# One core, a hybrid backbone block: the first down projection moved whole behind the first Strassen gate unit

## The chip, the cores and the metric

The kernel runs on one core of a Trainium2 chip. The metric is the device time of one execution in microseconds (us). Before the change it is 2523.57 us, the median of three runs (2523.08 to 2524.18). Views of the profile come from one profiled execution of the same kernel, which took 2524.79 us and whose instructions span 2523.1 us.

## The reference, cut to what matters

The block runs once (DEPTH = 1) on 512 tokens of width 2048. Two groups of recurrent heads, an output projection and a norm come first; the change touches only the channel mixer at the end:

```python
def conv_ffn(h, rows, cols, w_up, conv_w, conv_b, w_down):
    u = jnp.einsum('btd,df->btf', h, w_up)
    u_gate, u_val = jnp.split(u, 2, axis=-1)
    g = lax.conv_general_dilated(u_gate.reshape(b, rows, cols, D_FF), conv_w[:, :, None, :], ...
                                 feature_group_count=D_FF)
    g = g.reshape(b, t, D_FF) + conv_b
    return jnp.einsum('btf,fd->btd', jax.nn.silu(g) * u_val, w_down)
...
x = x + gt2 * conv_ffn(h2, rows, GRID_W, w_up, conv_w, conv_b, w_down)
return rmsnorm(x, g_final)
```

The inner width D_FF is 5504, that is 43 blocks of 128. The grid is 8 rows by 64 columns, and the convolution is 3x3 on each channel by itself.

## The kernel before, in words

All data lie with channels on the 128 partitions and the 512 tokens along the free dimension. Every product in float32 is made of three matrix products of parts: `split` copies a tile into a rounded `hi` on ScalarE (ACT, line 90) and takes the rest as `lo` on VectorE (DVE, line 91), and `mm3` (line 105) multiplies hi by hi, hi by lo and lo by hi. Weights come by DMA from the SP queue into four `raw` buffers and are split from there into two buffers for `hi` and two for `lo`, so that the DVE and ACT work for a weight chunk can run at most two chunks ahead of TensorE (PE).

The 43 blocks are cut into 11 groups (`QUADS`): group 0 has three blocks, the others four. A group q goes through four steps: the gate half of the up projection (`up_gate`, tile name ug), the convolution with its Silu (`convolve`, tile cv), the value half (`up_val`, tile uv) which is multiplied into the convolution's result and split (`product`, tiles gh and gl), and the down projection of these blocks (`down_sums`, tile dn). Down projections work in four blocks of 512 output channels; each block uses four PSUM banks, whose sums ACT scales into a staging tile `st` (line 1265) and a DMA from GpSimd's queue (POOL, line 1266) adds into the array x2d in HBM. The staging tiles come from a pool of three buffers.

Group 0 uses plain products (`unit`): per half 144 matmuls 512 wide, in three banks. Groups 1 to 10 use Strassen's scheme in a variant with seven products (`seven`: seven of the eight PSUM banks, 336 matmuls 256 wide per half), whose sums are put together by `four`: one copy on ACT and seven additions on DVE, in which the tiles u, v and t hold what is between. For this scheme the input tokens are needed in sums and differences as well: `token_sums(j)` and `token_last(j)`, j from 0 to 7, make them from the modulated tokens, and `token_last(j)` writes over a part of the operand that the plain products of group 0 read.

The SBUF tiles of this stage are sixteen named slots of one buffer each, y0 to y15 (`ytile(k, ...)`): two tiles in one slot exclude each other in time. First they hold the tokens x2; later u is y9, v is y11 and t is y13, convolution results are y8, y10, y12, y14, products y0 to y7. For group 0 the slots are written out by hand: the convolution results in y8, y9 and y13, the products gh and gl of its three blocks in y11 and y12, y15 and y7, y4 and y5.

The order on each engine's queue is fixed when the program is built: a planner takes, at each step of its own estimate of time, the ready instruction that comes first; program order sets the rank, and what stands under `tc.high_priority()` is ranked ahead. Engines then execute their queues strictly in order. On PE the order around the change is, from lines 1268 to 1285:

```python
up_gate(0)
...
convs = convolve(0); token_sums(2); up_val(0, convs)
...
down_sums(0, (0, 1), True)
for q in range(1, NQ):
    up_gate(q)
    down_sums(q - 1, (2, 3) if q == 1 else range(3) if q == NQ - 1 else range(4))
    up_val(q, convolve(q))
```

So the gate of group 0, the value of group 0, two blocks of down projection 0, the gate of group 1, the other two blocks of down projection 0, the value of group 1, the gate of group 2, and from there on down, value, gate in turn.

Of the kernel before, what the change touches and what calls it, by code (L numbers as in the profile page):

```python
# [11 lines left out]
F32 = mybir.dt.float32  # L12
F32R = mybir.dt.float32r
# [5 lines left out]
P = 128  # L19
HW = 256  # L20
D = 2048
KT = D // P
KP = KT // 2
T = 512
# [14 lines left out]
NQ = len(QUADS)  # L39
# [31 lines left out]
def block_kernel(ctx: ExitStack, tc: tile.TileContext, a: dict, out: bass.AP):  # L71
    nc = tc.nc
    V, S, G, PE = nc.vector, nc.scalar, nc.gpsimd, nc.tensor
# [9 lines left out]
    def mul(o, x, y):  # L83
        V.tensor_tensor(out=o, in0=x, in1=y, op=ALU.mult)
# [4 lines left out]
    def split(hi, lo, x):  # L89
        S.copy(hi, x)  # L90
        return V.tensor_tensor(out=lo, in0=x, in1=hi.bitcast(F32), op=ALU.subtract).ins  # L91
# [49 lines left out]
    def acc(name, shape=(P, T)):  # L141
        return (banks8[0] if banks8 else psA).tile(list(shape), F32, name=name, tag="acc")
# [5 lines left out]
    def ytile(k, name, shape=(P, T), dtype=F32):  # L148
        return yp.tile(list(shape), dtype, name=name, tag=f"y{k}")
# [56 lines left out]
    def unit_steps(src, name, xh, xl, accs, late=False, rates=None):  # L206

        n = len(accs)
        for kp in range(KP):
            if rates:  # L210
                rate[0] = rates[kp]
            wh, wl = load_split(src[kp], f"{name}_{kp}", w=P * n)
            if kp == 0 and late:

                for m, (ws, xs) in enumerate(((wh, xh), (wl, xh), (wh, xl))):
                    for k in range(2):
                        for i in range(n):
                            mm(accs[i], ws[:, k, P * i : P * i + P], xs[k], start=(m == 0 and k == 0), stop=False)
                continue
            for i in range(n):  # L220
                for kk in range(2):
                    k = 2 * kp + kk
                    mm3(accs[i], wh[:, kk, P * i : P * i + P], wl[:, kk, P * i : P * i + P],
                        xh[k], xl[k], k == 0, k == KT - 1)
                yield 1.36

    def unit(src, name, xh, xl, n=4, late=False, rates=None):

        accs = [acc(f"{name}_{i}") for i in range(n)]
        for _ in unit_steps(src, name, xh, xl, accs, late, rates):  # L230
            pass
        return accs
# [260 lines left out]
    cv = xp.tile([P, 32], F32, name="cv")  # L493
# [76 lines left out]
    for c0, n, hs, m in ((0, T, hx, gm[0]), (T, TC, hc, gm[1])):  # L570
        ps = psb(f"gm{c0}", (P, n))
        for k in range(KT):
            g = 32 * (k % 4)
# [417 lines left out]
    for h in range(1, 2 * H):  # L991
        if h + 1 < 2 * H:
            accs = [acc(f"a{h + 1}_{g}", BANKS[g]) for g in range(6)]
            steps = project_steps(h + 1, accs)
        else:
            rate[0] = 1.5
            accs = [acc(f"ga0_{i}") for i in range(4)]
# [16 lines left out]
    for g in range(4):  # L1014
        if g:
            accs = unit(a["w_gates"][g], f"ga{g}", *hx)
        for i in range(4):
            k = 4 * g + i
# [54 lines left out]
    for n in range(4):  # L1073
        pinned[0] = n == 3
        accs = unit(a["w_out"][n], f"wo{n}", yh, yl)
# [8 lines left out]
    with tc.high_priority():  # L1084
        _, r2 = token_rstd(sums2, rp, "rms2", idle=4)
# [12 lines left out]
    stp = pool(ctx, "stp", 3, waits="tile")  # L1098

    def operand(j, part, what, name, shape, dtype=F32R):  # L1100
        return bp.tile(list(shape), dtype, name=name, tag=f"b{part}{what}{j}")
# [6 lines left out]
    h2 = [[flat(b[k // 2][:, 2 * (k % 2) : 2 * (k % 2) + 2, :]) for k in range(KT)] for b in bq]  # L1108
# [15 lines left out]
    def token_sums(j):  # L1124

        k0, k1 = 2 * j, 2 * j + 1
        for k in (k0, k1):
            S.activation(x2[k], x2[k], AF.Identity, bias=modc[3][:, k : k + 1])
        sub(half(k0, 0), half(k0, 1), half(k0, 0))
        sub(half(k0, 1), half(k0, 1), half(k1, 1))  # L1130
        sub(half(k1, 1), half(k1, 1), half(k0, 0))
        split(flat(bt[0][j][:, 0:2, :]), flat(bt[1][j][:, 0:2, :]), x2[k0])
        sub(rest(j), half(k1, 1), half(k1, 0))
        split(bt[0][j][:, 2, :], bt[1][j][:, 2, :], half(k1, 1))
# [11 lines left out]
    gs = {}  # L1146
# [4 lines left out]
    def seven(src, name):  # L1151

        ps = [acc(f"{name}_{n}", (P, 2, HW)) for n in range(7)]
        for kp in range(KP):
            w = load_sums(src[kp], f"{name}_{kp}")
            for o, (g, s, b, c) in zip(ps, PRODUCTS):
                for m in range(2):
                    ms = slice(P * m, P * m + P)
                    mm3(o[:, m, :], w[g][0][:, s, ms], w[g][1][:, s, ms], b[0][kp][:, c, :], b[1][kp][:, c, :],
                        kp == 0 and m == 0, kp == KP - 1, skip_group_check=True)  # L1160
        return ps

    def four(ps, name, put):

        p1, p2, p4, p6, p7, p5, p3 = ps
        u, v = ytile(9, f"u_{name}", (P, 2, HW)), ytile(11, f"v_{name}", (P, 2, HW))
        with tc.high_priority():
            S.copy(u, p1)
            put(0, 0, u, p2, ALU.add)
            sub(u, u, p6)  # L1170
            sub(v, p7, u)
            put(1, 0, v, p4, ALU.subtract)
            put(1, 1, v, p5, ALU.add)
            sub(u, u, p5)
            put(0, 1, u, p3, ALU.add)

    def first_f(q):
        return 4 * q - 1 if q else 0
# [15 lines left out]
    def convolve(q):  # L1194
        convs = []
        for i in range(QUADS[q]):
            f = first_f(q) + i
            t = ytile((8, 9, 13)[i] if q == 0 else 8 + 2 * i, f"cv{f}")
            t3 = t.rearrange("p (r c) -> p r c", c=GW)
            for tap in range(9):  # L1200
                src = pads[:, i, tap // 3 : tap // 3 + ROWS, tap % 3 : tap % 3 + GW]
                w = cwt[:, f, tap : tap + 1]
                if tap == 0:
                    S.activation(t3, src, AF.Identity, scale=w, bias=cbt[:, f : f + 1])
                else:
                    V.scalar_tensor_tensor(out=t3, in0=src, scalar=w, in1=t3, op0=ALU.mult, op1=ALU.add)  # L1206
            S.activation(t, t, AF.Silu)
            convs.append(t)
        return convs

    def up_val(q, convs):

        def product(i):
            if q == 0:
                gh, gl = (ytile((11, 12, 15, 7, 4, 5)[2 * i + n], f"g{p}{i}", dtype=F32R) for n, p in enumerate("hl"))
            elif q == NQ - 1:
                gh, gl = (operand(4 + i, p, "t", f"g{p}{first_f(q) + i}", (P, T)) for p in "hl")
            else:
                gh, gl = (ytile(2 * i + n, f"g{p}{first_f(q) + i}", dtype=F32R) for n, p in enumerate("hl"))
            split(gh, gl, convs[i])  # L1220
            gs[first_f(q) + i] = (gh, gl)

        if q == 0:
            accs = unit(a["w_up3"][1], "uv0", *h2, n=3)
            with tc.high_priority():
                for i, ps in enumerate(accs):
                    mul(convs[i], convs[i], ps)
                    product(i)
        else:
            def put(mh, th, x, ps, op):  # L1230
                t = ytile(13, f"t{q}_{mh}{th}", (P, 2, HW))
                V.tensor_tensor(out=t, in0=x, in1=ps, op=op)  # L1232
                for i in range(2):
                    c = convs[2 * mh + i][:, HW * th : HW * th + HW]
                    mul(c, c, t[:, i, :])
                if (mh, th) in ((1, 1), (0, 1)):
                    for i in range(2):
                        product(2 * mh + i)

            four(seven(a["w_up4"][2 * q - 1], f"uv{q}"), f"uv{q}", put)  # L1240

    def down_block(q, blk, by_f=False):
        accs = [acc(f"dn{q}_{blk}_{i}") for i in range(4)]
# [13 lines left out]
    def down_sums(q, blks, by_f=False):  # L1257

        for blk in blks:
            accs = down_block(q, blk, by_f and blk == blks[0])  # L1260
            with tc.high_priority():
                for i in range(4):
                    k = 4 * blk + i
                    t = stp.tile([P, T], F32, name=f"st{q}_{k}", tag="st")
                    S.activation(t, accs[i], AF.Copy, scale=modc[5][:, k : k + 1])  # L1265
                    nc.gpsimd.dma_start(x2d[k], t, accum_op=ALU.add)  # L1266

    up_gate(0)
    st_p.close()
    banks8.append(pool(ctx, "psM", 8, PSUM, waits="tile"))  # L1270
    for j in reversed(range(3, KP)):
        token_sums(j)
    convs = convolve(0)
    token_sums(2)
    up_val(0, convs)
    for j in (1, 0):
        token_sums(j)
    for j in range(KP):
        token_last(j)
    down_sums(0, (0, 1), True)  # L1280
    for q in range(1, NQ):
        up_gate(q)
        down_sums(q - 1, (2, 3) if q == 1 else range(3) if q == NQ - 1 else range(4))
        up_val(q, convolve(q))
    down_sums(NQ - 2, (3,))

# [1 line left out]
    q = NQ - 1  # L1288
# [16 lines left out]
    for blk in range(3):  # L1305
        accs = down_block(q, blk)
# [38 lines left out]
    for hf, sl in enumerate(halves):  # L1345
# [4 lines left out]
        for at, (n, i) in enumerate(order):  # L1350
# [5 lines left out]
            gh, gl = gs[fs[n]]  # L1356
# [7 lines left out]
    with tc.high_priority():  # L1364
        _, r3 = root
# [67 lines left out]
```

## Time and profile before

| what | number |
|---|---|
| median of three runs | 2523.57 us |
| profiled execution, own time | 2524.79 us |
| its span, first to last instruction | 2523.1 us |
| PE busy | 2474.2 us (98%) |
| DVE busy | 1815.5 us (72%) |
| ACT busy | 1023.7 us (41%) |
| POOL busy | 182.8 us (7%) |
| DMA moved | 372.19 MB, mean 148 GB/s |

The rest, 1.7 us, lies around the span. The page of the profile names busy time by engine, the chain of work that ended last, and groups of instructions by line, engine and tile. A stretch of the trace is told as A:B in us from the span's start, with the busy time of each engine in it, the number of its instructions, the TensorE clock that was granted (1.00 is full speed) and the share of the DMA engines. A row of waits reads: who waited, for whom, us in total, how many times, the longest.

### The profile page before, as it was taken

What the parts mean: (1) busy time and instruction counts of PE and PEld (TensorE: products, weight loads), DVE (VectorE), ACT (ScalarE), POOL (GpSimd) and SP (SyncE); (2) the same over time, 40 slices, a digit from 0 to 9 for tenths busy, and PEclk for the clock granted to TensorE, in tenths of its full rate; (3) what the DMA queues carried; (4) which work ended last, traced back from release to release, by engine and by line L of the source; (5) the groups of instructions that cost most, each with busy time, mean ns of one, the idle gap of its engine ahead of it and who ended that gap; (6) DMA issues with size and microseconds to landing.
All of it is one profiled execution on the core that took longest, in us unless ns stands there. A gap on an engine that the chain in (4) does not pass through costs nothing.

```text
span 2523.1 us, 39365 instructions
## 1 busy us (share of the span) xinstructions
PE 2474.2 (98%) x15740; PEld 2207.8 (88%) x15740; DVE 1815.5 (72%) x2880; ACT 1023.7 (41%) x1514; POOL 182.8 (7%) x242
## 2 busy tenths in 40 slices
PE   6999999999999999999999999999999999999998
PEld 4887889888987888888899898999999999999997
DVE  6666754554445877848869888878787878787886
ACT  4224543332223233226543544444444444444445
POOL 0000000000000000000110202020201010101022
PEclk9999999999999999999999999999999999999999
DMA  9751011123334878842552737373737373736464
GB/s 382 269 173 41 26 43 51 55 79 118 115 112 162 290 275 303 298 144 98 138 130 94 174 101 167 101 173 96 174 101 167 106 168 105 165 109 159 114 187 134
DMA packets 121551, 372.19 MB, mean 148 GB/s; under 512 B 13908, under 2 KB 18328, under 8 KB 121368
## 3 DMA queue, kind: packets, MB, share of 16 engines
q1 hardware_dynamic: 94680, 318.29, 37.6%
q0 software_dynamic: 25600, 50.34, 11.7%
q8 instruction: 123, 2.02, 0.3%
q10 hardware_dynamic: 1088, 1.05, 0.1%
q14 instruction: 60, 0.49, 0.1%
HBM read 319.30 MB, written 50.33 MB: 146 GB/s over the span
## 4 chain that ended last, share of the span: by engine, by line
PE 90%; DVE 4%; issue 3%; DMA 2%; ACT 1%; POOL 0%; SPq 0%; DVEq 0%; POOLq 0%; ACTq 0%
PE a L96 19%; PE dn L96 17%; PE uv L96 16%; PE ug L96 15%; PE ga L96 7%; PE wo L96 7%; PE po L96 4%; PE sl L96 1%; PE ps_m L96 1%; DMA raw_m<-in_w_mod 1%; PE cst L96 1%; PE s L96 1%; DVE cv L1206 0%; DMA xl<-in_xT 0%; DVE sum_ug L87 0%
## 5 line engine op out<-in xcount | busy, mean ns | idle before, releaser
L96 PE MATMUL dn<-gh,hi_d 128*128 128x512 f32 x672 | 261.7, 389 | 2.3 <-ACT st L1265 2.3
L96 PE MATMUL dn<-gh,lo_d 128*128 128x512 f32 x672 | 261.6, 389 | 0.1
L96 PE MATMUL dn<-gl,hi_d 128*128 128x512 f32 x672 | 261.6, 389 | 0.0
L1206 DVE SCALAR_TENSOR_TENSOR cv<-pads,cwt,cv 128x512 f32<-128x512 f32 x344 | 239.2, 744 | 0.6
L1266 POOL DMA_DIRECT2D x2d<-st x160 | 140.3, 916 | 1153.7 <-ACT st L1265 1149.4
L304 DVE SCALAR_TENSOR_TENSOR sum_m<-raw_m,csil,sum_m 128x512 f32<-128x512 f32 x240 | 180.0, 750 | 10.4 <-DMA raw_m<-in_w_mod 4.5
L91 DVE TENSOR_TENSOR lo_buv<-sum_uv,hi_buv 128x1024 fp32r<-128x1024 f32 x80 | 97.9, 1223 | 107.9 <-ACT hi_buv L90 102.5
L1265 ACT ACTIVATE st<-dn,mod 128x512 f32<-128x512 f32 x160 | 108.6, 689 | 120.6 <-DMA x2d<-st 92.0
L96 PEld LDWEIGHTS dn<-gh,hi_d 128*128 128x128 f32 x672 | 126.2, 188 | 28.5 <-ACT st L1265 2.9
L96 PE MATMUL a<-hi_h,hTh 128*128 128x256 f32 x512 | 150.4, 294 | 0.5 <-ACT e L397 0.5
L96 PEld LDWEIGHTS dn<-gh,lo_d 128*128 128x128 f32 x672 | 126.2, 188 | 26.9 <-DVE lo_d L91 0.7
L96 PEld LDWEIGHTS dn<-gl,hi_d 128*128 128x128 f32 x672 | 126.2, 188 | 26.1 <-DVE gl L91 0.2
L96 PE MATMUL a<-hi_h,hTl 128*128 128x256 f32 x512 | 144.7, 283 | 0.0
L96 PE MATMUL a<-lo_h,hTh 128*128 128x256 f32 x512 | 144.7, 283 | 0.0
L96 PE MATMUL ug<-bth,hi_bug 128*128 128x256 f32 x480 | 136.8, 286 | 2.0 <-DVE t L1232 1.1
L96 PE MATMUL ug<-bql,hi_aug 128*128 128x256 f32 x480 | 136.1, 284 | 0.0
L96 PE MATMUL ug<-bqh,lo_aug 128*128 128x256 f32 x480 | 136.1, 284 | 0.0
L96 PE MATMUL ug<-bqh,hi_aug 128*128 128x256 f32 x480 | 136.0, 284 | 0.0
L90 ACT CAST hi_d<-raw_d 128x1024 fp32r<-128x1024 f32 x86 | 88.7, 1031 | 116.6 <-PE ug L96 71.0
L96 PE MATMUL uv<-bqh,lo_auv 128*128 128x256 f32 x480 | 135.8, 283 | 0.0
L96 PE MATMUL uv<-bth,hi_buv 128*128 128x256 f32 x480 | 135.8, 283 | 0.0
L96 PE MATMUL uv<-btl,hi_buv 128*128 128x256 f32 x480 | 135.8, 283 | 0.0
(378 smaller groups left out, 7342.7 us busy)
## 6 DMA issues: line engine op xcount, KB each, us to landing
raw_m<-in_w_mod SPq DMA_DIRECT2D x192, 512.0 KB, 5.2
raw_d<-in_w_down SPq DMA_DIRECT2D x82, 512.0 KB, 3.4
raw_ug<-in_w_up SPq DMA_DIRECT2D x80, 512.0 KB, 3.5
x2d<-st POOLq DMA_DIRECT2D x160, 256.0 KB, 5.3
raw_uv<-in_w_up SPq DMA_DIRECT2D x80, 512.0 KB, 5.3
raw_h<-in_w_heads SPq DMA_DIRECT2D x64, 512.0 KB, 3.6
raw_ga<-in_w_gates SPq DMA_DIRECT2D x32, 512.0 KB, 4.5
raw_wo<-in_w_out SPq DMA_DIRECT2D x32, 512.0 KB, 4.7
```

The source lines that it names most:

```text
L90: S.copy(hi, x)
L91: return V.tensor_tensor(out=lo, in0=x, in1=hi.bitcast(F32), op=ALU.subtract).ins
L96: ins = PE.matmul(*args, **kw)
L304: V.scalar_tensor_tensor(out=parts[0], in0=x, scalar=ck, in1=parts[0], op0=ALU.mult, op1=ALU.add)
L1206: V.scalar_tensor_tensor(out=t3, in0=src, scalar=w, in1=t3, op0=ALU.mult, op1=ALU.add)
L1265: S.activation(t, accs[i], AF.Copy, scale=modc[5][:, k : k + 1])
L1266: nc.gpsimd.dma_start(x2d[k], t, accum_op=ALU.add)
```

## The change

Five things are done. The sums of the value half of group 0 are no longer multiplied into the convolution from PSUM: ACT copies them (`vals`, in y0, y1, y3), and the multiplication, on DVE as before, reads the copy. The convolution of group 0 and its products stand behind this in program order, and all eight `token_sums` stand ahead of the value half. Down projection 0 has its four blocks together, behind the gate of group 1. The down sums get a fourth staging buffer: the last of each block's four sums goes to y15, or y0 for group 0. The slots of group 0 change: its second convolution result moves from y9 to y12, its products from y11, y12, y15, y7, y4, y5 to y4, y5, y7, y15, y2, y6; and the three banks of its value half are taken in reverse order.

```diff
-            t = ytile((8, 9, 13)[i] if q == 0 else 8 + 2 * i, f"cv{f}")
+            t = ytile((8, 12, 13)[i] if q == 0 else 8 + 2 * i, f"cv{f}")
...
+    def product(q, convs, i):
+        if q == 0:
+            gh, gl = (ytile((4, 5, 7, 15, 2, 6)[2 * i + n], f"g{p}{i}", dtype=F32R) for n, p in enumerate("hl"))
...
+        split(gh, gl, convs[i])
+        gs[first_f(q) + i] = (gh, gl)
...
-                gh, gl = (ytile((11, 12, 15, 7, 4, 5)[2 * i + n], f"g{p}{i}", dtype=F32R) for n, p in enumerate("hl"))
...
-            accs = unit(a["w_up3"][1], "uv0", *h2, n=3)
-            with tc.high_priority():
-                for i, ps in enumerate(accs):
-                    mul(convs[i], convs[i], ps)
-                    product(i)
...
-                    t = stp.tile([P, T], F32, name=f"st{q}_{k}", tag="st")
+                    name = f"st{q}_{k}"
+                    t = ytile(15 if q else 0, name) if i == 3 else stp.tile([P, T], F32, name=name, tag="st")
...
-    for j in reversed(range(3, KP)):
+    for j in reversed(range(KP)):
         token_sums(j)
-    convs = convolve(0)
-    token_sums(2)
-    up_val(0, convs)
-    for j in (1, 0):
-        token_sums(j)
+    vals = []
+    accs = [acc(f"uv0_{i}") for i in range(3)][::-1]
+    for _ in unit_steps(a["w_up3"][1], "uv0", *h2, accs):
+        pass
+    for i, ps in enumerate(accs):
+        vals.append(ytile((0, 1, 3)[i], f"uv0s{i}"))
+        with tc.high_priority():
+            S.copy(vals[i], ps)
     for j in range(KP):
         token_last(j)
-    down_sums(0, (0, 1), True)
+    convs = convolve(0)
+    for i in range(3):
+        mul(convs[i], convs[i], vals[i])
+        product(0, convs, i)
     for q in range(1, NQ):
         up_gate(q)
-        down_sums(q - 1, (2, 3) if q == 1 else range(3) if q == NQ - 1 else range(4))
+        down_sums(q - 1, range(3) if q == NQ - 1 else range(4), q == 1)
         up_val(q, convolve(q))
```

More of the change, by code (lines that the diff above doesn't have):

```diff
@@ L1209, in convolve, with put @@
         return convs
-    def up_val(q, convs):
-        def product(i):
-            if q == 0:
-                gh, gl = (ytile((11, 12, 15, 7, 4, 5)[2 * i + n], f"g{p}{i}", dtype=F32R) for n, p in enumerate("hl"))
[L1216 to L1223, printed above, removed]
-            accs = unit(a["w_up3"][1], "uv0", *h2, n=3)
-            with tc.high_priority():
-                for i, ps in enumerate(accs):
-                    mul(convs[i], convs[i], ps)
-                    product(i)
[L1229 to L1232, printed above, removed]
-                for i in range(2):
[L1234 to L1240, printed above, removed]
+    def product(q, convs, i):
+        if q == 0:
+            gh, gl = (ytile((4, 5, 7, 15, 2, 6)[2 * i + n], f"g{p}{i}", dtype=F32R) for n, p in enumerate("hl"))
+        elif q == NQ - 1:
+            gh, gl = (operand(4 + i, p, "t", f"g{p}{first_f(q) + i}", (P, T)) for p in "hl")
+        else:
+            gh, gl = (ytile(2 * i + n, f"g{p}{first_f(q) + i}", dtype=F32R) for n, p in enumerate("hl"))
+        split(gh, gl, convs[i])
+        gs[first_f(q) + i] = (gh, gl)
+    def up_val(q, convs):
+        def put(mh, th, x, ps, op):
+            t = ytile(13, f"t{q}_{mh}{th}", (P, 2, HW))
+            V.tensor_tensor(out=t, in0=x, in1=ps, op=op)
+            for i in range(2):
+                c = convs[2 * mh + i][:, HW * th : HW * th + HW]
+                mul(c, c, t[:, i, :])
+            if (mh, th) in ((1, 1), (0, 1)):
+                for i in range(2):
+                    product(q, convs, 2 * mh + i)
+        four(seven(a["w_up4"][2 * q - 1], f"uv{q}"), f"uv{q}", put)
     def down_block(q, blk, by_f=False):
```

## The prediction

> **What bounds the kernel now.** I read the page's busy times and chain first.
>
> ```profile
> span 2523.1 us, 39365 instructions
> PE 2474.2 (98%) x15740; PEld 2207.8 (88%) x15740; DVE 1815.5 (72%) x2880; ACT 1023.7 (41%) x1514; POOL 182.8 (7%) x242
> PE 90%; DVE 4%; issue 3%; DMA 2%; ACT 1%; POOL 0%; SPq 0%; DVEq 0%; POOLq 0%; ACTq 0%
> ```
>
> PE is busy 98% of the span. The change adds and removes no matmul, so it can only win or lose time in which PE waits or runs below its pace. I therefore cut the trace at the borders of PE's own sections. The rows are, in order: gate 0, value 0, down 0 blocks 0 and 1, gate 1, down 0 blocks 2 and 3, value 1, gate 2; then, for comparison, a value and a gate half later on and three blocks of down 9, which have as many matmuls as the whole of down 0 (144; the counts are one or two higher where a window cuts a neighbour's).
>
> ```profile
> core 0: us, PE busy (x) PEld busy (x) DVE busy (x) ACT busy (x) POOL busy (x), PEclk, DMA share, GB/s
> 1150.28:1184.58 34.30, 32.95 (x144) 26.92 (x144) 34.27 (x59) 30.50 (x49) 0.00 (x0) 1.00 0.26 81
> 1184.58:1217.38 32.80, 32.78 (x144) 27.14 (x145) 32.74 (x57) 18.19 (x31) 0.00 (x0) 1.00 0.28 85
> 1217.38:1233.89 16.51, 16.51 (x73) 13.36 (x72) 13.04 (x27) 8.97 (x14) 3.61 (x4) 1.00 0.63 178
> 1233.89:1278.32 44.43, 42.19 (x337) 41.77 (x336) 26.97 (x38) 16.20 (x19) 3.49 (x4) 0.96 0.50 122
> 1278.32:1297.62 19.30, 16.97 (x74) 13.29 (x73) 10.24 (x16) 7.93 (x11) 3.54 (x4) 1.00 0.71 185
> 1297.62:1337.93 40.31, 40.31 (x337) 40.29 (x336) 38.05 (x60) 21.09 (x26) 3.48 (x4) 1.00 0.51 123
> 1337.93:1383.85 45.92, 42.33 (x338) 40.79 (x337) 43.86 (x70) 17.20 (x21) 0.00 (x0) 1.00 0.25 81
> 1427.40:1467.71 40.31, 40.31 (x337) 40.30 (x336) 28.65 (x41) 16.61 (x19) 2.42 (x3) 1.00 0.45 115
> 1467.71:1508.21 40.50, 40.50 (x338) 40.36 (x337) 32.95 (x52) 15.88 (x19) 0.00 (x0) 1.00 0.32 104
> 2379.04:2411.71 32.67, 32.67 (x146) 27.04 (x145) 30.63 (x45) 18.46 (x24) 7.90 (x9) 1.00 0.77 180
> ```
>
> The stretch up to the end of gate 2 takes 34.30 + 32.80 + 16.51 + 44.43 + 19.30 + 40.31 + 45.92 = 233.57 us. The same matmuls at the later pace would take 32.95 + 32.80 + 40.50 + 32.67 + 40.31 + 40.50 = 219.73 us. The difference, **13.84 us**, is all that the change can win here: 1.35 at the end of gate 0, 3.93 in gate 1, 16.51 + 19.30 - 32.67 = 3.14 in down 0, 5.42 in gate 2. The later rows have PE busy throughout, so no section can go below them. The waits of PE in that stretch name what stands in front:
>
> ```profile
> PE dn L96 <- ACT st L1265: 2.3, 1, 2.3
> PE ug L96 <- ACT st L1265: 2.2, 2, 1.7
> PE ug L96 <- DVE u_uv L81: 1.6, 1, 1.6
> PE uv L96 <- ACT pads L1185: 1.4, 1, 1.4
> PE ug L96 <- DVE t L1232: 0.9, 1, 0.9
> PE ug L96 <- DVE lo_bug L91: 0.6, 1, 0.6
> PE ug L96 <- ACT hi_bug L90: 0.3, 1, 0.3
> ```
>
> Nearly all are waits for a PSUM bank: for a down sum that ACT has not yet copied (st), for sums of value 1 that DVE has not yet put together (u, t), for the gate copy (pads). Why these are late shows in the instructions of v of gate 1 (first row) and the waits of other engines, within 1278 to 1300 (next two) and within gate 2 (last):
>
> ```profile
> L81 DVE TENSOR_TENSOR v_ug<-ug,u_ug x1: 692/692/692, 1294.4 to 1294.4; 128x512 f32<-128x512 f32 x1
> ...
> DVE v_ug L81 <- PE dn L96: 5.7, 1, 5.7
> ACT st L1265 <- DMA x2d<-st: 6.4, 4, 4.6
> ...
> ACT hi_aug L90 <- DVE cv L1206: 5.4, 1, 5.4
> ```
>
> v of gate 1 is slot y11, and y11 still holds gh of block 0 until the last block of down 0 has read it. So DVE cannot put gate 1 together before 1294.4, the convolution of group 1 starts some 15 us late, runs into value 1 (DVE 38.05 of 40.31 there) and is not done when gate 2 wants the banks.
>
> **The change part by part.**
>
> *Gate 0 to value 0 (1.35).* Value 0's first bank waits for the last of three copies (0.59 us each, below). Taken in reverse, that bank is wanted two accumulators later, 2/3 of the way into the first chunk's 4.1 us (32.80 / 8), that is 2.7 us on, when the copy is done. Left: 0 (bounds 0 and 1.35; the copy ends 1.4 us after gate 0, nearer the first).
>
> *The copies of the value sums.* They are three ACT copies from PSUM, like this row:
>
> ```profile
> L1185 ACT COPY pads<-ug 128x512 f32<-128x512 f32 x3 | 1.8, 590 | 1.5 <-PE ug L96 1.5
> ```
>
> 3 x 0.59 = 1.8 us on ACT, which was busy 18.19 of 32.80 us in value 0. Gate 1 can take five of its banks at once; the sixth is wanted five products of 40.31 / 56 = 0.72 us later, 3.6 us, and the last copy is due 0.6 us after value 0. Cost 0; without that cover it would be 0.6, and behind the copies on ACT's queue stand the casts for gate 1, which run up to two chunks ahead. The multiplications and the products stay on DVE, at the same count.
>
> *Gate 1 directly after value 0 (3.93).* Its waits for st vanish, since no down sums stand ahead. They were 2.24 us (44.43 less 42.19); the other 1.69 us is slower matmuls, and the granted clock shows it:
>
> ```profile
> 1234.00:1242.00 8.00, 5.76 (x42) 5.36 (x41) 3.52 (x7) 3.25 (x5) 2.51 (x3) 0.91 1.03 219
> 1242.00:1250.00 8.00, 8.00 (x61) 8.00 (x61) 7.50 (x11) 3.89 (x5) 0.98 (x2) 0.88 0.72 140
> ```
>
> 8 x 0.09 + 8 x 0.12 = 1.68 us. I take it that the clock fell for the idle time and stays up without it. The Trainium skill (TensorE: Matmul & The Clock Gate, Part 1) says that the clock falls after a whole idle window of about 3.4 us; the idle here is shorter. By that rule the drop would have another cause and might stay, a rival below.
>
> What is new is DVE's load. Gate 1 needs all token sums from DVE first, and DVE still owes the convolution of group 0, which used to run in value 0:
>
> ```profile
> 1174.20:1217.38 43.18, 41.82 (x184) 34.28 (x183) 43.10 (x81) 25.71 (x45) 0.00 (x0) 1.00 0.29 91
> 1174.20:1233.89 59.69, 58.33 (x256) 47.64 (x255) 56.14 (x107) 34.68 (x59) 3.61 (x4) 1.00 0.38 115
> ...
> L1206 DVE SCALAR_TENSOR_TENSOR cv<-pads,cwt,cv 128x512 f32<-128x512 f32 x24 | 16.7, 744 | 0.0
> L91 DVE TENSOR_TENSOR lo_d<-raw_d,hi_d 128x1024 fp32r<-128x1024 f32 x2 | 2.4, 1218 | 0.0
> L91 DVE TENSOR_TENSOR gl<-cv,gh 128x512 fp32r<-128x512 f32 x3 | 2.0, 681 | 0.0
> L84 DVE TENSOR_TENSOR cv<-cv,uv 128x512 f32<-128x512 f32 x3 | 2.0, 676 | 0.0
> L91 DVE TENSOR_TENSOR lo_d<-raw_d,hi_d 128x512 fp32r<-128x512 f32 x2 | 1.4, 688 | 0.0
> ```
>
> From 1174.20, where the token sums begin, to the end of gate 1 DVE has to do 56.14 + 26.97 (the gate 1 row) less 2.4 + 1.4 for down weights that now come later, 79.3 us. It has from 1174.20 to 1183.2 + 32.80 + 40.50 = 1256.5, that is 82.3 us. It fits, at 96%. Token sums rank ahead of the convolution, so gate 1 starts on time and the convolution fills the gaps. What such filling costs PE is shown by two rows: value 1, with DVE at 94%, lost nothing; gate 2, at 96%, lost 5.42, but mostly for banks that DVE itself had to free, which gate 1 does not wait for. Left in gate 1: **1.0** (bounds 0 and 5.4).
>
> *Down 0 in one piece (3.14).* With products in y4, y5, y7, y15, y2, y6, slot y11 is free and DVE puts gate 1 together at its end. The products must be ready: the first at once, the third after 24 matmuls at 32.67 / 144 = 0.227 us, 5.4 us later. Then there is DMA. Four blocks of 8.17 us (32.67 / 4) now follow each other, each with four accumulating transfers:
>
> ```profile
> q0 software_dynamic: 1855, 3.39, 48.2%
> q1 hardware_dynamic: 1440, 5.24, 37.2%
> ```
>
> These are the transfers within down 1 (1384 to 1428, 44 us): x2d's queue took 21.2 us of all engines for 3.39 MB, 6.3 us per MB, the weights 16.4 us for 5.24 MB, 3.1 per MB. Down 0 has 16 sums of 0.262 MB (26.2 us), 3.15 MB of weights (9.8) and the first four loads of value 1 (2.10 MB, 6.5). Four raw buffers (1.57 MB, 4.9) can be filled in gate 1, and the last block's sums (6.6) may land under value 1: 31.0 us in 32.67. It just fits, and the fourth staging buffer lets a whole block's sums be under way. A sum has a block's 8.17 us to leave its bank before PE wants it. Left in down 0, with products perhaps late: **1.8** (bounds 0, as in the row of down 9 at a DMA share of 0.77, and 5.0, all 37.7 us of DMA less 32.67).
>
> *SP and POOL.* SP issues the eight loads of gate 1 ahead of down 0's eight instead of behind its first four; gate 1's come into an idle queue (share 0.28). POOL's first eight sums come some 60 us later; nothing else stands in its queue. Both 0.
>
> *Value 1 and gate 2 (5.42).* The convolution of group 1 takes 32 taps, 16.7 / 24 x 32 = 22.3 us, and starts with down 0 instead of 3 us before its end; it is done early in value 1, whose own DVE work fills 28.65 of 40.31 later on. So gate 2 finds its banks free as gate 3 does (40.50). Left: 0.3 in value 1, **0.4** in gate 2 (bounds 0 and 5.42; nearest is gate 3, whose value half follows its down projection in the same way).
>
> *The fourth buffer later on.* ACT waits long for landings:
>
> ```profile
> L1265 ACT ACTIVATE st<-dn,mod 128x512 f32<-128x512 f32 x160 | 108.6, 689 | 120.6 <-DMA x2d<-st 92.0
> ```
>
> But PE waits for none of this after gate 2, so it saves 0; a sum in y15 waits only for the landing of the block before, as the ring does now. Its slot has no other user there; y0, which holds down 0's, is wanted next by the products at the end of value 1.
>
> **The sum.** 13.84 - (1.0 + 1.8 + 0.3 + 0.4) = 10.3 us less. The profiled execution would go from 2524.79 to 2514.5, and the median, 1.2 lower, from 2523.57 to **2513.3 us**. The least possible is 2523.57 - 13.84 = 2509.7.
>
> **The rivals.**
> - *DMA is the bound of down 0.* Its price is the upper end, 5.0 in place of 1.8: 2516.5. For it: st waited up to 4.6 us for landings with blocks as short as these. Against: down 1 carries the same sums with PE busy throughout.
> - *The token sums come late.* Before, DVE did all 24 taps by 1217 and had 13.0 us (56.14 - 43.10) left, 2.7 of it products and 2.6 down weights: 7.7 us of tokens and gate 1's first chunk. In that order gate 1 would start 7.7 us late, with 1.7 for the clock: 2523.57 - 13.84 + 7.7 + 1.7 + 1.0 = 2520. Against: program order now has the tokens ahead.
> - *The convolution of group 0 starves* (slower). Ranked last, it gets only what gate 1's casts leave; DVE's queue is fixed by estimates, and if the taps are queued behind waits for PE, they remain at gate 1's end. Then down 0 has no products, and gate 1's sums cannot go to pads, which the taps still read: PE stands for up to 16.7 + 2.0 + 2.0 = 20.7 us, plus 1.7 for the clock: 2523.57 - 13.84 + 20.7 + 1.7 + 1.7 = 2534. It ends slower once more than about 15 of the 20.7 us are left. Against: DVE did 43.10 of 43.18 us in this place before, and the value 1 row shows it filling gaps to 94%.
> - *The clock drop stays*: if the 0.91 and 0.88 have another cause than the idle time, the 1.7 us in gate 1 is not won, 2515. Against: the drop follows the waits at once. For: gate 2 has 3.59 us of idle time (45.92 less 42.33) at 1.00. The clock gate page, as cited above, speaks for it.
>
> **How the numbers follow.** A measurement of this kernel can tell about 0.2%, 5 us, from no change. My forecast (2510 to 2516, with the clock rival inside it) has a chance of 0.58, DMA 0.13, late tokens 0.15, starved convolution 0.10, none of these 0.04. Faster by over 0.2% (below 2518.5): 0.58, most of DMA's, some of the tokens': 0.74. Within 0.2%: 0.14. Slower: 0.12. The range goes from the least possible to the late tokens with some DMA loss on top: 2509.5 to 2522.5.
>
> **What would show it.** Right: PE's order is gate 0, value 0, gate 1, down 0 with 144 matmuls, value 1, gate 2; v of gate 1 waits for no down matmul; gate 2 takes about 40.5 us; the clock is 1.00 in gate 1. Wrong: PE in gate 1 waits for token splits (bt, bq), in down 0 for gh, gl or st, or in value 1 for st. The prediction fails if gate 1 and down 0 together lose more than 9 us, or if PE waits in a down projection after gate 2.

## The result and the profile after

The changed kernel takes 2519.64 us (median of 21 runs, 2516.80 to 2522.34) against 2524.22 us (21 runs, 2522.73 to 2526.07) of the kernel before on the same chips: 4.6 us less, a ratio of 0.9982 with a 95% interval of 0.9976 to 0.9987. The gain is real, but at 0.18% it lies just within the 0.2% that the prediction called the limit, and it is less than half of the 10.3 us forecast. The profiled execution took 2519.45 us.

The head of the page of the changed kernel: the span and the busy times.

```profile
span 2517.7 us, 39396 instructions
PE 2474.2 (98%) x15740; PEld 2207.1 (88%) x15740; DVE 1816.2 (72%) x2880; ACT 1024.1 (41%) x1517; POOL 183.0 (7%) x242
```

Busy times hardly moved, as they should when no matmul is added or removed; the three new ACT instructions are the copies. The sections of PE, in the new order gate 0, value 0, gate 1, down 0, value 1, gate 2 (same columns as in the prediction):

```profile
core 0: us, PE busy (x) PEld busy (x) DVE busy (x) ACT busy (x) POOL busy (x), PEclk, DMA share, GB/s
1149.93:1184.27 34.34, 32.97 (x144) 26.91 (x144) 34.30 (x59) 30.52 (x49) 0.00 (x0) 1.00 0.25 81
1184.27:1217.06 32.79, 32.78 (x144) 27.15 (x145) 32.75 (x64) 19.77 (x33) 0.00 (x0) 1.00 0.41 132
1217.06:1257.37 40.31, 40.31 (x337) 40.30 (x336) 35.66 (x54) 17.45 (x22) 0.00 (x0) 1.00 0.25 78
1257.37:1296.58 39.21, 35.78 (x146) 28.59 (x145) 33.38 (x50) 21.20 (x31) 11.21 (x13) 0.91 0.74 172
1296.58:1336.90 40.32, 40.32 (x337) 40.30 (x336) 31.36 (x47) 17.19 (x21) 2.92 (x4) 1.00 0.54 135
1336.90:1377.41 40.51, 40.51 (x338) 40.38 (x337) 32.95 (x52) 15.89 (x19) 0.00 (x0) 1.00 0.32 104
```

They add up to 227.48 us, 6.1 less than the 233.57 before. Gate 1, value 1 and gate 2 run without a gap. Two sections do not: gate 0, and above all down 0 with 39.21 us, of which 35.78 are busy. The waits of PE in this stretch:

```profile
PE dn L96 <- ACT hi_d L90: 3.4, 1, 3.4
PE uv L96 <- ACT pads L1185: 1.4, 1, 1.4
```

The 1.4 us at the end of gate 0 is the old one. The 3.4 us is new: PE waits for the cast of a chunk of down weights. What that one wait does to the pace of PE shows in three windows of 8 us in down 0:

```profile
1273.00:1281.00 8.00, 8.00 (x37) 6.60 (x37) 6.21 (x9) 4.57 (x7) 3.49 (x4) 1.00 1.04 232
1281.00:1289.00 8.00, 4.57 (x13) 2.87 (x12) 5.39 (x10) 4.62 (x7) 2.62 (x3) 0.71 0.57 102
1289.00:1297.00 8.00, 8.00 (x34) 6.56 (x33) 6.57 (x10) 2.74 (x4) 1.79 (x3) 0.87 1.06 293
```

The clock falls from 1.00 to 0.71 and 0.87; these are averages, and in shorter windows it reads 0.50 from 1284.31 to 1291.13 and 1.00 on both sides. So down 0 lost 39.21 - 35.78 = 3.4 us idle and, against the 32.67 of three blocks at full pace, 35.78 - 32.67 = 3.1 us in slower matmuls. ACT's own instructions, in order of time, with the idle time before each in brackets, show why the cast came late:

```profile
1278.76 0.84 ACT L90 CAST hi_auv<-raw_uv 128x768 fp32r<-128x768 f32 x1 [0.94 <-DMA raw_uv<-in_w_up]
1283.61 0.83 ACT L90 CAST hi_auv<-raw_uv 128x768 fp32r<-128x768 f32 x1 [4.01 <-DMA raw_uv<-in_w_up]
1284.35 1.04 ACT L90 CAST hi_d<-raw_d 128x1024 fp32r<-128x1024 f32 x1
```

ACT did nothing for 4.01 us, while the cast that PE needed (hi_d) stood behind a cast that nobody needed yet: hi_auv, of the second weight chunk of value 1, whose load had not landed. That load was issued at 1276.5 and landed at 1283.6. DVE stood behind the same load:

```profile
1283.61 0.69 DVE L87 TENSOR_TENSOR sum_uv<-raw_uv 128x512 f32<-128x512 f32 x1 [3.02 <-DMA raw_uv<-in_w_up]
```

The `lo` of the same chunk of down weights came behind this row on DVE, at 1285.42. All loads of value 1's weights issued from 1270 to 1300 took this long (least, median, most):

```profile
DMA to landing us min/median/max: 7.1/8.4/9.7
```

After gate 2 something is given back. The changed kernel reaches the end of gate 2 6.4 us earlier than the one before (1377.41 against 1383.85), but its span ends 5.4 us earlier. The 1.0 us goes in the later down projections, where four blocks took 43.55 us before (1383.85 to 1427.40): down 1 takes 43.81 now, others up to 44.03. Six of them lose 1.4 us in all, and a gate half that was 0.3 us longer before gives a part back. The same shape of loss stands there, smaller, and here on DVE's queue. One row of DVE in down 3, first of the changed kernel and then the same place in the kernel before:

```profile
1657.88 0.69 DVE L87 TENSOR_TENSOR sum_uv<-raw_uv 128x512 f32<-128x512 f32 x1 [3.30 <-DMA raw_uv<-in_w_up]
```

```profile
1661.53 0.69 DVE L87 TENSOR_TENSOR sum_uv<-raw_uv 128x512 f32<-128x512 f32 x1 [1.02 <-DMA raw_uv<-in_w_up]
```

There the order is the same in both kernels: a lo_d, the `lo` of down weights, comes right behind this row. The load merely lands later, and the cover of one chunk ahead is used up: PE's next matmul with that lo_d starts 0.45 us after the one before it instead of 0.227. The list of PE's waits has no entry for so short a delay.

### The profile page after: what moved, and what is told of

Read it like the earlier page. It is cut to its first block, busy times and chain, and to the rows that moved or that the text cites. A ratio compares the mean times of both kernels' runs of the same rounds, so it can differ in the third digit from the quotient of the medians.

```text
span 2517.7 us, 39396 instructions
## 1 busy us (share of the span) xinstructions
PE 2474.2 (98%) x15740; PEld 2207.1 (88%) x15740; DVE 1816.2 (72%) x2880; ACT 1024.1 (41%) x1517; POOL 183.0 (7%) x242
## 4 chain that ended last, share of the span: by engine, by line
PE 86%; issue 9%; DMA 2%; DVE 2%; ACT 1%; POOL 0%; SPq 0%; DVEq 0%; ACTq 0%; POOLq 0%
PE a L96 19%; PE dn L96 16%; PE uv L96 16%; PE ug L96 14%; PE ga L96 7%; PE po L96 4%; PE wo L96 3%; PE sl L96 1%; PE ps_m L96 1%; DMA raw_uv<-in_w_up 1%; DMA raw_m<-in_w_mod 1%; PE cst L96 1%; PE s L96 1%; DMA xl<-in_xT 0%; DMA x2d<-st 0%
## 5 line engine op out<-in xcount | busy, mean ns | idle before, releaser
L91 DVE TENSOR_TENSOR lo_d<-raw_d,hi_d 128x1024 fp32r<-128x1024 f32 x86 | 102.7, 1194 | 48.7 <-ACT hi_d L90 48.0
L96 PE MATMUL uv<-bth,lo_buv 128*128 128x256 f32 x480 | 135.8, 283 | 0.0
L96 PE MATMUL uv<-bql,hi_auv 128*128 128x256 f32 x480 | 135.8, 283 | 0.0
```

The costliest lines, as they stand in the source:

```text
L96: ins = PE.matmul(*args, **kw)
```

## The experiments

The first theory (A) was that down 0 loses its 6.5 us to the order on ACT's queue, because the load lands late beside the accumulating transfers. Its rivals: down 0 is bound by the throughput of DMA, or by the staging buffers. Two smaller questions were asked beside it: why the 1.4 us after gate 0 stayed, and whether slot y11 was the cause of gate 2's loss before. Where nothing else is said, a run is compared with the kernel before on the same chip, and section lengths are those of one profiled execution, which can lie some 2 us from the median of its run.

**The casts of value 1 behind those of down 0.** The first two chunks of value 1's weights are summed and split only after the last hi and lo of down 0 have been issued on their engines. This is the changed kernel with:

```diff
-        S.copy(hi, x)
+        last_cast[0] = S.copy(hi, x).ins
...
-    def load_sums(src, name):
+    def load_sums(src, name, behind=()):
...
-        with tc.high_priority():
+        with tc.high_priority(), ExitStack() as held:
+            for ins in behind:
+                held.enter_context(tc.issue_after(ins))
...
-            w = load_sums(src[kp], f"{name}_{kp}")
+            w = load_sums(src[kp], f"{name}_{kp}", behind if kp < 2 else ())
...
-        four(seven(a["w_up4"][2 * q - 1], f"uv{q}"), f"uv{q}", put)
+        behind = (last_cast[0], parted[0]) if q == 1 else ()
+        four(seven(a["w_up4"][2 * q - 1], f"uv{q}", behind), f"uv{q}", put)
```

> The changed kernel, with one thing more: the casts and splits of value 1's first two weight chunks stand behind those of down 0's last block on ACT's and DVE's queues. Theory A (the cast hi_auv of value 1's second chunk waits for its load and holds up the last block's hi_d behind it): down 0 takes about 33 us instead of 39.2, the 3.4 us wait of PE for hi_d is gone and the clock stays at 1.00, so about 6 us less than the changed kernel's 2519.6, that is 2513.5. Theory B (down 0 is bound by its sums' transfers, whatever the order): PE waits for st instead, in the last block or in value 1, and the time stays within 1.5 us of 2519.6.

Measured: 2515.11 us (five runs) against 2524.70, a ratio of 0.9959 (0.9945 to 0.9973), 9.6 us less. Down 0 and value 1 by windows, then the waits of PE from gate 0 to the first later down projection, and the cast of hi_d that had come at 1284.35:

```profile
1257.16:1290.34 33.18, 32.98 (x146) 26.97 (x145) 30.65 (x47) 19.32 (x28) 9.97 (x12) 1.00 0.79 172
1290.34:1331.68 41.34, 40.56 (x337) 40.35 (x336) 33.56 (x50) 19.17 (x24) 4.07 (x5) 1.00 0.61 158
```

```profile
PE uv L97 <- ACT pads L1188: 1.4, 1, 1.4
PE uv L97 <- DVE lo_buv L91: 0.8, 1, 0.8
PE dn L97 <- DVE lo_d L91: 0.2, 1, 0.2
...
1278.98 1.05 ACT L90 CAST hi_d<-raw_d 128x1024 fp32r<-128x1024 f32 x1 [1.65 <-PE dn L97]
```

The cast can run at 1278.98, so in the changed kernel it must have been ready while ACT stood idle, from 1279.6 to 1283.6. Down 0 goes from 39.21 to 33.18 us with the clock at 1.00, at a higher DMA share (0.79 against 0.74). So the transfers fit, as the prediction had it, and throughput is not what held down 0. The edit orders ACT's and DVE's queues together; what each was worth is not shown. Value 1 gives back 1.0 us, as its first chunks now come late for itself. The later down projections, which this edit leaves alone, still lose (up to 45.09 us).

**No accumulating transfers in the first three blocks of down 0.** This leaves 12 of the 16 sums of down 0 out of the output; what it takes away is 12 x 256 KB of traffic in that place.

```diff
-                    nc.gpsimd.dma_start(x2d[k], t, accum_op=ALU.add)
+                    if q or blk == 3:
+                        nc.gpsimd.dma_start(x2d[k], t, accum_op=ALU.add)
```

> The changed kernel without the accumulating transfers of down 0's first three blocks (12 sums are scaled but not added, so that part of the output's sum is left out); the order on all engines as it was. Theory A1 (the load of value 1's second chunk lands late because the sums' transfers share the DMA engines with it): it lands in about 3.5 us instead of 7, hi_auv waits under 1 us, and down 0 takes about 33 us. Theory A2 (the load lands late because SP issues it late, at 1276.5, when the raw buffer comes free): the wait of hi_auv stays at 3 us or more and down 0 over 37 us.

Measured: 2515.50 us (a single run) against 2524.24. Down 0 by windows, the landing of value 1's loads from 1270 to 1300, and ACT's cast of the same second chunk:

```profile
1257.10:1290.52 33.42, 32.96 (x146) 26.96 (x145) 32.51 (x49) 20.98 (x31) 0.62 (x1) 1.00 0.40 129
...
DMA to landing us min/median/max: 3.5/4.3/5.7
...
1279.61 0.84 ACT L90 CAST hi_auv<-raw_uv 128x768 fp32r<-128x768 f32 x1 [1.90 <-DMA raw_uv<-in_w_up]
```

The order of the casts is that of the changed kernel, and still the loss in down 0 is nearly gone: the load lands in 4.3 us at the median instead of 8.4, and ACT waits 1.90 us for it instead of 4.01, which PE's supply covers but for 0.5. That load itself landed in 4.3 us instead of 7.1; the rest of the 4.0 us by which the cast comes earlier is its issue, at 1275.2 instead of 1276.5. Together with the run above this shows both halves of the cause: the order puts the wanted cast behind a load, and the accumulating transfers make that load late. Either alone costs little (33.42 and 33.18 in down 0, against 32.67).

**Without the fourth staging buffer.**

```diff
-                    t = ytile(15 if q else 0, name) if i == 3 else stp.tile([P, T], F32, name=name, tag="st")
+                    t = stp.tile([P, T], F32, name=name, tag="st")
```

> The changed kernel without the fourth staging buffer. If the fourth buffer is what brings the loads of value 1 late (more sums in flight at once): down 0 gets shorter than 39.2 us, and the later down projections, which took up to 44.0 us in the changed kernel, take 43.55 again; 2514 to 2518. If it does what it was given for: the fourth sum of each block waits about 4 us on ACT for a landing, casts stand behind it, and down 0 takes as long or longer; 2519 to 2524.

Measured: 2520.59 us (11 runs) against 2524.70, 0.9982 (0.9973 to 0.9991), 4.1 us less, where the changed kernel has 4.6. Down 0, value 1, and two waits of PE:

```profile
1258.71:1297.79 39.08, 34.75 (x146) 27.88 (x145) 33.45 (x50) 19.40 (x28) 10.61 (x12) 0.96 0.73 165
1297.79:1339.85 42.06, 40.83 (x337) 40.41 (x336) 31.30 (x47) 18.82 (x23) 3.48 (x4) 1.00 0.57 137
...
PE dn L96 <- ACT hi_d L90: 4.3, 1, 4.3
PE uv L96 <- ACT st L1259: 1.2, 2, 0.8
```

Down 0 loses as much as with four buffers, in a wait for the same cast. But here ACT first stood 2.88 us until a staging tile had landed, and then 1.71 us for the load. In the profile the fourth buffer saves 1.7 us in value 1 (42.06 against 40.32), which otherwise waits for down sums that ACT could not yet copy. By the medians it is worth about 0.5 us in this form of the kernel, less than these intervals can tell.

**Only slot y11 made free.** This is the kernel *before*, with v of gate 1 in slot y14, which nobody holds then.

```diff
-        u, v = ytile(9, f"u_{name}", (P, 2, HW)), ytile(11, f"v_{name}", (P, 2, HW))
+        u, v = ytile(9, f"u_{name}", (P, 2, HW)), ytile(14 if name == "ug1" else 11, f"v_{name}", (P, 2, HW))
```

> The kernel before, with only v of gate 1 moved from slot y11 to y14. Theory A (in the kernel before the waits behind gate 1 come from y11, still held by gh): v of gate 1 is made at about 1277 instead of 1294, the second half of down 0 takes 16.5 to 17.5 us (19.30), gate 2 41 to 42 (45.92), and the time is 6 to 7 us under the kernel before, 2517.5. Theory B (the convolution of group 1 comes late because only half of down 0 covers it): gate 2 stays over 44 us and the time is 2 to 3 us under, 2521.5.

Measured: 2521.66 us (11 runs) against 2524.70, 0.9988 (0.9979 to 0.9996), 3.0 us less. v of gate 1, then the second half of down 0, value 1 and gate 2, and two waits of PE in gate 2:

```profile
L81 DVE TENSOR_TENSOR v_ug<-ug,u_ug x1: 692/692/692, 1277.2 to 1277.2; 128x512 f32<-128x512 f32 x1
...
1278.38:1294.76 16.38, 16.38 (x74) 13.53 (x73) 14.97 (x25) 9.96 (x14) 3.54 (x4) 1.00 0.66 171
1294.76:1336.53 41.77, 40.82 (x337) 40.40 (x336) 38.42 (x59) 19.48 (x24) 3.48 (x4) 1.00 0.56 134
1336.53:1381.67 45.14, 42.73 (x338) 42.02 (x337) 38.64 (x61) 16.30 (x20) 0.00 (x0) 0.96 0.30 94
...
PE ug L96 <- DVE u_uv L81: 2.1, 1, 2.1
PE ug L96 <- DVE t L1232: 0.3, 1, 0.3
```

v now stands at 1277.2 instead of 1294.4, and the second half of down 0 gains 2.9 us (19.30 before). But value 1 takes 1.5 more (40.31 before), and gate 2 gets only 0.8 faster (45.92 before). So the late v explained the gap in down 0, and not gate 2. What gate 2 lacked, it seems, is time for DVE between gate 1 and value 1: in this order half a down projection, some 16 us, where the later groups have a whole one of 43.55. The changed kernel gives it a whole down 0, and gate 2 then takes 40.51. No run tests this by itself.

**One more PSUM bank for gate 0.** The idle products ahead of gate 0 take two banks instead of one.

```diff
-        idle_products(acc("idle", (P, P)), sums2[0][:, 0:P], 7)
+        idle_products(acc("idle", (P, P)), sums2[0][:, 0:P], 4)
+        idle_products(acc("idle2", (P, P)), sums2[0][:, 0:P], 3)
```

> The changed kernel, with the idle products ahead of gate 0 spread over two banks, which moves gate 0's accumulators on by one bank, so that its last one is not in the bank that value 0 takes first. If that bank is why value 0 still starts 1.35 us late: the wait of PE for pads goes, 1.3 us less, about 2518.3. If value 0 waits for all three copies in any case: the wait stays 1.4 us and the time is that of the changed kernel, 2519.6.

Measured: 2518.90 us (11 runs) against 2524.70, 0.9979 (0.9970 to 0.9988); against the changed kernel's 2519.64 that is too little to tell. In the profile the wait is gone. Gate 0 and value 0, and the only wait of PE that is left up to gate 2 beside a 0.2:

```profile
1149.94:1182.70 32.76, 32.76 (x147) 27.13 (x146) 32.13 (x56) 27.98 (x45) 0.00 (x0) 1.00 0.26 82
1182.70:1215.34 32.64, 32.64 (x145) 27.03 (x144) 32.63 (x65) 20.27 (x36) 0.00 (x0) 1.00 0.43 136
...
PE dn L96 <- ACT hi_d L90: 3.3, 1, 3.3
```

The start of value 0 tells why. In the kernel before, its first matmul starts at 1184.60, right after the third copy of gate 0's sums has ended (1184.55). In the changed kernel it does so again (1184.28 after 1184.22), although the accumulators are taken in reverse. Here it starts at 1182.71, while the third copy ends at 1184.19. So in both kernels the accumulator that PE uses first had the bank that gate 0 filled last, and with one bank shifted it finds one that is free. A likely reason is that banks are given out in the order of first use on PE, so that reversing the order of use reversed the banks with it; no profile here names the banks, so this is not shown.

**Both repairs, for all groups.** The second-bank edit, and the edit of the first experiment with `if q` in place of `if q == 1`:

```diff
-        behind = (last_cast[0], parted[0]) if q == 1 else ()
+        behind = (last_cast[0], parted[0]) if q else ()
```

> The changed kernel with the first two chunks of every value half put behind the last down block before it, as for value 1 alone in the run that did so, and with the spare bank. If the later down projections' 0.3 to 1.5 us come from the same queueing (an addition or cast of value's second chunk ahead of the last block's split): each takes 43.55 us again, value 1 keeps its 41.3, gate 0 loses its 1.35: 2512.3. If they come from something else, 2 to 3 us more.

Measured: **2510.33 us** (five runs, 2508.10 to 2510.82) against 2524.24, a ratio of 0.9945 (0.9932 to 0.9957): 13.9 us less than before, and 9.3 less than the changed kernel. Gate 0 to gate 2:

```profile
1147.91:1180.69 32.78, 32.77 (x144) 27.10 (x145) 32.76 (x57) 28.99 (x46) 0.00 (x0) 1.00 0.27 82
1180.69:1213.33 32.64, 32.64 (x145) 27.03 (x144) 32.57 (x64) 20.11 (x35) 0.00 (x0) 1.00 0.45 136
1213.33:1253.64 40.31, 40.31 (x337) 40.30 (x336) 37.33 (x57) 17.86 (x24) 0.00 (x0) 1.00 0.26 77
1253.64:1286.58 32.94, 32.94 (x146) 26.97 (x145) 30.95 (x48) 19.53 (x28) 10.57 (x12) 1.00 0.82 181
1286.58:1326.89 40.31, 40.31 (x337) 40.30 (x336) 33.34 (x49) 18.96 (x24) 3.48 (x4) 1.00 0.57 156
1326.89:1367.40 40.51, 40.51 (x338) 40.38 (x337) 32.96 (x52) 15.89 (x19) 0.00 (x0) 1.00 0.33 102
```

Together 219.49 us, 0.2 below the floor that the prediction worked out (219.73), as gate 1 takes 40.31 instead of 40.50. No section waits, the clock is 1.00, and every later down projection of four blocks takes 43.55 us again. Down 0 carries all its sums at a DMA share of 0.82 without loss.

**Only the second chunk held back.** As above, but `behind if kp == 1 else ()`, so that the first chunk of value q keeps its place ahead of the last down cast.

> As the run before, but only the second chunk of every value half stands behind the last down block; the first keeps its place. The held-up load was the second chunk's, so down 0 should take 33 us as well and the later ones 43.55, while value 1, whose first chunk is now split early, should lose 0.0 to 0.5 us instead of 1.0: 2511.5. If the first chunk's load is late too, down 0 takes 34 us or more and this run is slower than the one before.

Measured: 2512.25 us (five runs) against 2524.24, 0.9951 (0.9937 to 0.9964). Down 0, and the wait of PE in it:

```profile
1255.97:1291.13 35.16, 33.25 (x146) 26.88 (x145) 32.16 (x49) 20.79 (x30) 10.56 (x12) 1.00 0.81 180
...
PE dn L97 <- DVE lo_d L91: 1.8, 1, 1.8
```

In down 0 the first chunk's load is late as well: 2.2 us more than with both held back (35.16 against 32.94). The later down projections take 43.55 us, so there one chunk is enough.

**Both repairs, with three buffers.** The kernel of 2510.33 us without the fourth staging buffer (the edit shown above).

> The kernel with the first two chunks of every value half behind the last down block and the spare bank, but with three staging buffers instead of four. If the fourth buffer serves down 0 only (the run with three buffers lost 1.7 us more in value 1): value 1 takes 41.5 to 42 us instead of 40.3, down 0 33 to 34, the later sections stay at 43.55 and 40.31, and the time is 1.5 to 2.5 us above the kernel with four, 2512.5. If it serves nothing once the queues are in order: the same time, 2510.3.

Measured: 2515.30 us (six runs) against 2525.09, 0.9967 (0.9955 to 0.9980): 9.8 us less than before instead of 13.9. Down 0 and value 1, then the waits of ACT for staging tiles from 1250 to 1300 and the waits of PE:

```profile
1255.11:1291.82 36.71, 34.78 (x146) 28.00 (x145) 32.44 (x49) 20.76 (x30) 10.85 (x13) 0.95 0.81 172
1291.82:1332.21 40.39, 40.39 (x337) 40.35 (x336) 31.87 (x48) 17.62 (x21) 3.20 (x4) 1.00 0.56 147
...
ACT st L1264 <- DMA x2d<-st: 14.2, 10, 4.5
...
PE dn L97 <- DVE lo_d L91: 1.1, 1, 1.1
PE dn L97 <- ACT hi_d L90: 0.8, 1, 0.8
```

Neither expectation held. By the medians the fourth buffer is worth about 4 us once the casts are in order (the two intervals just touch), and the loss is in down 0 (36.71 against 32.94), not in value 1. With three, ACT's copies of the down sums wait longer for staging tiles to land (10.0 us from 1253 to 1292, against 3.0 with four), and casts of down weights stand behind these copies: the same queue, blocked by another transfer. That is not all of it. The hi_d that PE waited for, at 1279.54, stood behind a copy that had waited 2.67 us for PE's own sums, and its lo_d behind eight convolution steps on DVE; how the 3.8 us divide is open.

## Why the prediction was right or wrong

The direction was right and the time is in the range; the size was not. By the prediction's own terms, what is left of each loss:

| step | forecast left, us | measured left, us |
|---|---|---|
| gate 0 to value 0 | 0 (0 to 1.35) | 34.34 - 32.95 = 1.39 |
| gate 1 | 1.0 (0 to 5.4) | 40.31 - 40.50 = -0.19 |
| down 0 in one piece | 1.8 (0 to 5.0) | 39.21 - 32.67 = 6.54 |
| value 1 | 0.3 | 0.01 |
| gate 2 | 0.4 (0 to 5.42) | 0.01 |
| later on | 0 | 1.0 |

In the stretch 3.5 us were to be left, and 7.75 are. Three steps failed. The time lies close to the 2520 that the prediction gave for late token sums; that is an accident, as no such delay occurred.

*"Down 0 in one piece" is the step that decides*, and it lies above its upper bound. The bound came from throughput: 37.7 us of transfers against 32.67. What counted was the latency of one load and what stood behind it on the queues of ACT and DVE. The prediction counted the transfers and never asked how long a single load of value 1 takes to land among them, nor in which order ACT and DVE split the weights there: PE waited 3.4 us for hi_d and lost 3.1 more in pace. Its signs of being wrong do not name this either: in down 0 they have PE wait for gh, gl or st, and the 6.35 us that gate 1 and down 0 lost together stay below their 9. With the casts in order the same transfers cost 0.3 us (32.94 against 32.67), so the estimate "it just fits" held; the rival "DMA is the bound" falls with it. The fourth buffer, which the prediction credited with letting a block's sums be under way, is needed for that: 3.8 us in this section.

*"Gate 0 to value 0: left 0"* failed entirely: the wait of 1.4 us stayed. It took the reversed order to put another bank first, but value 0 again started right after the third copy; one bank more removed the wait.

*"The fourth buffer later on", saving 0,* holds for the buffer. But the forecast that nothing is lost after gate 2 does not: 1.0 us was, in the later down projections, by splits behind late loads. With three buffers two of them were as long (44.03 and 44.31 in that run), so the fourth buffer alone is not the reason; why value 1's and later loads land later than before the change there (a median of 7.0 us in the stretch of down 3 against 6.0) stays open.

*Gate 1* came out better than forecast: PE waits for nothing and the clock is 1.00. The drop to 0.91 and 0.88 before went with the idle time, and stayed with it in the run with y14 (0.92 and 0.87 in the same windows, PE busy for 5.70 of the first 8 us). So the rival "the clock drop stays" falls. The rivals "token sums late" and "convolution starves" fall by DVE's own instructions, the splits of the token sums (btl), of their last parts (bql) and of the products of group 0 (gl; least, median and longest duration in ns, first and last start):

```profile
L91 DVE TENSOR_TENSOR btl<-x,bth x16: 414/552/684, 1176.9 to 1196.4; 128x512 fp32r<-128x512 f32 x8, 128x256 fp32r<-128x256 f32 x8
...
L91 DVE TENSOR_TENSOR bql<-x,bqh x8: 415/418/423, 1196.8 to 1219.9; 128x256 fp32r<-128x256 f32 x8
```

```profile
L91 DVE TENSOR_TENSOR gl<-cv,gh x3: 684/686/692, 1242.1 to 1247.9; 128x512 fp32r<-128x512 f32 x3
```

The sums are done 20 us ahead of gate 1 (1217.06). Of the last parts, the last is split 2.8 us into it, and PE waits for none. The products are done 9 us ahead of down 0 (1257.37). DVE did find the room between; the estimate of 96% load was pessimistic only in what it took such filling to cost.

*Gate 2* came out as forecast (40.51 against 40.5), and for the reason given for the new order, as far as DVE's busy time in value 1 (31.36 of 40.32 us) tells. The reading of the kernel before was wrong in part: the chain from the late v through the convolution to gate 2 carries only 0.8 of its 5.4 us, as the run with y14 showed. *The copies of the value sums* cost nothing, as forecast.

## What to carry to other kernels

Engines here take their queues in order, so a sum of transfer times is not enough when a stage gets more DMA traffic: look at what stands in each engine's queue ahead of the operand that the bottleneck needs next, and price each such instruction by the landing time of its own load under the new traffic. Early casts for the next stage are safe only as long as their loads land early; holding them behind the last cast of the current stage cost at most 1 us where they were then late, and gained 6. Where accumulators are reordered to escape a bank, check which banks they get.

## What the runs showed of the hardware

- *A strict queue turns a late load into a stop of work that does not need it.* ACT stood 4.01 us with a ready cast behind the waiting one, and DVE 3.02 us at the same load. The Trainium skill (TensorE: Matmul & The Clock Gate, the table at its head) names the queues of ScalarE and VectorE strict FIFO; this trace agrees, with those 4.01 us.
- *Loads beside accumulating transfers land twice as late.* A load of 512 KB took 7.1 to 9.7 us to land in down 0, and 3.5 to 5.7 in the same place with 12 of the 16 accumulating transfers left out.
- *Idle time of PE can cost as much again in pace.* After 3.8 us from the start of the last matmul to the next (1281.66 to 1285.44), matmuls 512 wide started 0.59 to 0.67 us apart three times and then 0.427, in place of 0.227, until about 1291, and the section lost 3.1 us to it on top of 3.4 idle. The Trainium skill (TensorE: Matmul & The Clock Gate, Part 1) gives 426.7 ns as the pace of the throttled clock, which is what the trace shows. It also has the clock fall after a whole idle window of about 3.4 us; here PE was busy for a part of that time, and the clock fell all the same. In the changed kernel it was busy for 1.15 us of the 3.41 from 1280.90, and then the clock was 0.50 for 6.82 us. In gate 1 of the kernel before it was busy for 1.48 us of the 3.41 from 1237.15, with no idle piece over 1.7 us, and then the clock was 0.50 for 3.41 us; the 0.91 and 0.88 are averages over that.
- *The spread grew with the stall.* The changed kernel's 21 runs lie 5.5 us apart, the 21 of the kernel before 3.3. Those with both repairs lie 2.7 apart, but are only five. That fits a loss that depends on when single transfers land; no run tested it by itself.
